# Seven-product gate/up, paired squares, early inputs and TensorE modulation in a two-layer hybrid trunk

## The chip, the cores and the metric

The kernel runs on all eight cores of one Trainium2 chip (trn2), one sequence of the batch on each core. The metric is device time in microseconds (us) of the slowest core.

A program on all cores does not always run alike on this chip. In some runs the cores of one or both dies show a lower granted clock in the records and the time is longer; such runs are called slow. In the last job below, the kernel before took 2306 to 2310 us in its fast runs, with 0.972 to 0.978 of the clock on average on every core, and 2720.5 us in its slowest, with 0.81 on one die; half_products had a run of 2399 us with 0.89 to 0.91 on one die and 0.82 to 0.83 on the other.

## The reference, cut to what matters

```python
D_MODEL, BATCH, SEQ, DEPTH, D_FF = 1024, 8, 2048, 2, 2816

def rmsnorm(x, g):
    y = x * rsqrt(mean(x * x, -1) + EPS)
    return y * g

def modulate(x, g, mod):                 # mod = silu(c) @ w_mod + b_mod, one vector per sequence
    shift, scale, gate = split(mod, 3)
    return rmsnorm(x, g) * (1 + scale) + shift, gate

def swiglu(h, w_in, w_out):
    g, u = split(h @ w_in, 2)            # 1024 -> 2 x 2816
    return (silu(g) * u) @ w_out         # 2816 -> 1024

# each layer, each with its own shift, scale and gate:
#   x += 0.5 * gate * swiglu_1(h);  x += gate * mixer(h);  x += 0.5 * gate * swiglu_2(h)
# mixer: layer 0 spatial gating and short convolution, layer 1 causal pooling; a final rmsnorm
```

Four SwiGLUs of 2048 tokens carry most of the work. A modulation vector is the product of one 1024-vector with an fp32 matrix of 1024 by 3072 per sub-layer, handled as 24 rows of 128 x 1024 (512 KB each).

## The kernel before

Tokens lie in four tiles of 512. Activations are held feature by token: a matmul has 128 x 128 weights as the stationary operand and 512 tokens as the moving one. Gate/up is the plain product, eight chunks of the inner dimension for gate and eight for up:

```python
def ffn_inproj(l, i, j, kk, t, slot, mark=False):
    ...
    for c in range(NC):                                   # NC = 8
        add("pe", I("matmul", PS[bg][:], SL[:, slot, c*256:c*256+128], role.hbuf[:, c, tsl(t)], ...))
    for c in range(NC):
        add("pe", I("matmul", PS[bu][:], SL[:, slot, c*256+128:c*256+256], role.hbuf[:, c, tsl(t)], ...))
    sg = tp_rot.next()
    add("act", I("activation", out=TP[:, sg, 0:TT], in_=PS[bg][:], func=AF.Silu), ...)
    add("dve", I("tensor_tensor", out=role.abuf[:, kk, tsl(t)], in0=TP[:, sg, 0:TT], in1=PS[bu][:], op=ALU.mult), ...)
```

The mean square over features is a matmul with a matrix of ones, one matmul for each squared chunk:

```python
def stats_gen(t, res, rot=None, sq_pool=False):
    for c in range(NC):
        ...                                               # square X[c] on GpSimd or ScalarE into SQ[q]
        add("pe", I("matmul", PS[b][:], ONES[:], SQ[:, q, :], start=(c == 0), stop=(c == NC - 1)), ...)
```

All modulation rows are dot products on VectorE, one row of 128 x 1024 a step:

```python
def mod_step():
    ...
    add("dve", I("scalar_tensor_tensor", out=JUNK[:], in0=ap, scalar=1.0, in1=CB[:],
                 op0=ALU.mult, op1=ALU.mult, accum_out=MODT[:, q:q + 1]), ...)
```

Between sub-layers a boundary works through the four tiles in turn: output projection of a tile, its squares, its sum, its normalised input for the next sub-layer.

Of the kernel before, what the change touches and what calls it, by code (L numbers as in the profile page):

```python
# [5 lines left out]
F32 = mybir.dt.float32  # L6
# [8 lines left out]
NT = 4  # L15
# [3 lines left out]
GROUPS = [list(range(0, 8)), list(range(8, 15)), list(range(15, 22))]  # L19
EPS = 1e-6  # L20
N_SUB_RUN = 6
RUN_FINAL = True

class Op:
    __slots__ = ("idx", "eng", "fn", "cdeps", "ddeps", "semkey", "pos", "seq",
                 "signal", "dma_target")

class Sched:
    ENGS = ("pe", "act", "dve", "pool", "sp")
    WINDOW = 10 ** 9  # L30

    def __init__(self):
        self.ops = []
        self.lastw = {}
        self.rd_eng = {}
        self.rd_dma = {}
        self.npos = {e: 0 for e in self.ENGS}

    def add(self, eng, fn, reads=(), writes=(), dma=None):
        ops = self.ops  # L40
        idx = len(ops)
        deps = set()
        for k in reads:
            w = self.lastw.get(k)
            if w is not None:
                deps.add(w)
        for k in writes:
            w = self.lastw.get(k)
            if w is not None:
                deps.add(w)  # L50
            r = self.rd_eng.get(k)
            if r:
                deps.update(r.values())
            r = self.rd_dma.get(k)
            if r:
                deps.update(r)
        op = Op()
        op.idx = idx
        op.eng = eng
        op.fn = fn  # L60
        op.semkey = dma
        cd = {}
        dd = []
        for d in deps:
            o = ops[d]
            if o.semkey is not None:
                dd.append(d)
            elif cd.get(o.eng, -1) < d:
                cd[o.eng] = d
        op.cdeps = cd  # L70
        op.ddeps = dd
        op.pos = self.npos[eng]
        self.npos[eng] += 1
        op.signal = False
        op.seq = 0
        op.dma_target = 0
        ops.append(op)
        for k in reads:
            if dma is not None:
                self.rd_dma.setdefault(k, []).append(idx)  # L80
            else:
                self.rd_eng.setdefault(k, {})[eng] = idx
        for k in writes:
            self.lastw[k] = idx
            self.rd_eng[k] = {}
            self.rd_dma[k] = []
        return idx

    def _skip(self, op, o):
        if o.eng == op.eng and op.semkey is None:  # L90
            if o.eng == "pe":
                return True
            if op.pos - o.pos > self.WINDOW:
                return True
        return False

    def emit(self, nc, block):
        ops = self.ops
        for op in ops:
            for e, d in op.cdeps.items():  # L100
                o = ops[d]
                if not self._skip(op, o):
                    o.signal = True
        cnt = {e: 0 for e in self.ENGS}
        dcnt = {}
        for op in ops:
            if op.semkey is not None:
                dcnt[op.semkey] = dcnt.get(op.semkey, 0) + 16
                op.dma_target = dcnt[op.semkey]
            elif op.signal:  # L110
                cnt[op.eng] += 1
                op.seq = cnt[op.eng]
        self.sig_counts = cnt
        esem = {e: nc.alloc_semaphore("s_" + e) for e in self.ENGS}
        dsem = {k: nc.alloc_semaphore("d_%d" % i) for i, k in enumerate(dcnt)}
        self.n_sems = len(esem) + len(dsem)
        by_eng = {e: [] for e in self.ENGS}
        for op in ops:
            by_eng[op.eng].append(op)

        def run(eng_name, E):
            waited = {}
            for op in by_eng[eng_name]:
                for e, d in op.cdeps.items():
                    o = ops[d]
                    if not o.signal or self._skip(op, o):
                        continue
                    if waited.get(("e", e), 0) < o.seq:
                        E.wait_ge(esem[e], o.seq)
                        waited[("e", e)] = o.seq  # L130
                for d in op.ddeps:
                    o = ops[d]
                    if waited.get(("d", o.semkey), 0) < o.dma_target:
                        E.wait_ge(dsem[o.semkey], o.dma_target)
                        waited[("d", o.semkey)] = o.dma_target
                if op.fn is None:
                    continue
                ins = op.fn(E)
                if op.semkey is not None:
                    ins.then_inc(dsem[op.semkey], 16)  # L140
                elif op.signal:
                    ins.then_inc(esem[op.eng], 1)
# [11 lines left out]

SM_BMOD = 0
# [5 lines left out]
SM_BS = 224  # L161
SM_N = 736

def _blk(w, cols):
    return np.ascontiguousarray(w[:, cols].reshape(8, 128, -1).transpose(1, 0, 2))

def piece_plan():
    plan = []
    for l in range(2):
        for i in range(2):  # L170
            if i == 1:
                if l == 0:
                    plan += [("abv", 0), ("abv", 1), ("abu", 0), ("abu", 1)]
                    for hf in range(2):
                        plan += [("abb", 2, hf), ("abb", 3, hf), ("abb", 4, hf)]
                    plan += [("abo", dp) for dp in range(4)]
                else:
                    plan += [("pool",)]
            for g, ks in enumerate(GROUPS):
                for j in ks[:4]:  # L180
                    plan.append(("win", l, i, j))
                for dp in range(4):
                    plan.append(("wout", l, i, g, dp))
                for j in ks[4:]:
                    plan.append(("win", l, i, j))
    return plan

def build_pieces(inp):
    plan = piece_plan()
    out = np.zeros((len(plan), 128, 2048), np.float32)  # L190
    w_in = inp["w_ffn_in"]
    w_out = inp["w_ffn_out"]
# [3 lines left out]
    for n, p in enumerate(plan):  # L196
        k = p[0]
        if k == "win":
            _, l, i, j = p
            w = w_in[l, i]  # L200
            a = _blk(w, slice(j * 128, (j + 1) * 128))
            b = _blk(w, slice(D_FF + j * 128, D_FF + (j + 1) * 128))
            out[n] = np.concatenate([a, b], axis=2).reshape(128, 2048)
        elif k == "wout":
            _, l, i, g, dp = p
            w = w_out[l, i]
            ks = GROUPS[g]
            blk = np.zeros((128, 2, 8, 128), np.float32)
            for dd in range(2):
                for kk, kc in enumerate(ks):  # L210
                    blk[:, dd, kk, :] = w[kc * 128:(kc + 1) * 128, (2 * dp + dd) * 128:(2 * dp + dd + 1) * 128]
            out[n] = blk.reshape(128, 2048)
        elif k == "abv":
            hp = p[1]
            out[n] = _blk(abw, slice(512 + hp * 256, 512 + (hp + 1) * 256)).reshape(128, 2048)
        elif k == "abu":
            hp = p[1]
            blk = np.stack([_blk(abw, slice((2 * hp + ff) * 128, (2 * hp + ff + 1) * 128)) for ff in range(2)], axis=1)
            out[n] = blk.reshape(128, 2048)
        elif k == "abb":  # L220
            _, sec, hf = p
            base = sec * 512
            blk = np.stack([_blk(abw, slice(base + (2 * hf + ff) * 128, base + (2 * hf + ff + 1) * 128)) for ff in range(2)], axis=1)
            out[n] = blk.reshape(128, 2048)
        elif k == "abo":
            dp = p[1]
            blk = np.stack([_blk(abo, slice((2 * dp + dd) * 128, (2 * dp + dd + 1) * 128)) for dd in range(2)], axis=1)
            out[n] = blk.reshape(128, 2048)
        elif k == "pool":
            blk = np.zeros((128, 4, 2, 256), np.float32)  # L230
            for i in range(4):
                for kc in range(2):
                    blk[:, i, kc, :] = pw[i, kc * 128:(kc + 1) * 128, :]
            out[n] = blk.reshape(128, 2048)
    return out

def build_small(inp):
# [7 lines left out]
    sm[:, SM_BS:SM_BS + 512] = np.broadcast_to(inp["ab_b_s"][0].reshape(1, 512), (128, 512))  # L245
    return sm

def build_wmod(inp):
    wm = inp["w_mod"]
    return np.ascontiguousarray(wm.transpose(0, 2, 1).reshape(2 * 72, 128, 1024))  # L250
# [3 lines left out]

def build_nc(n_sub_run=N_SUB_RUN, run_final=RUN_FINAL):
    nc = bass.Bass("TRN2", target_bir_lowering=False)
    plan = piece_plan()
    xT = nc.dram_tensor("xT", [D, S], F32, kind="ExternalInput").ap()
    cb_d = nc.dram_tensor("cb", [128, D], F32, kind="ExternalInput").ap()
    small_d = nc.dram_tensor("small", [128, SM_N], F32, kind="ExternalInput").ap()  # L260
# [915 lines left out]
```

## Time and profile before

| | before |
|---|---|
| three runs | 2306.36, 2717.41, 2721.04 us |
| the profiled run (fast) | cores 2298.5 to 2309.1 us |
| TensorE busy (slowest core) | 2151 us, 93% |
| VectorE / ScalarE / GpSimd busy | 43% / 24% / 9% |
| first gate/up matmul | 65.5 us |

The stated median of three, 2717 us, is a slow run. The fast level is 2306.

The page of the kernel before, its parts on busy time, on the 40 slices (tenths busy; PEclk is the granted clock in tenths) and on the chain that ended last:

```profile
PE 2151.3 (93%) x10136; PEld 984.7 (43%) x10136; DVE 997.4 (43%) x1575; ACT 543.1 (24%) x855; POOL 211.0 (9%) x297
...
PE   0779999999899999999999999999997699999996
...
PEclk9889999999999999999999999999997899999998
...
PE 82%; DMA 6%; DVE 4%; ACT 3%; issue 3%; SPq 1%; POOL 0%; DVEq 0%; ACTq 0%; POOLq 0%
```

The row of TensorE says where the time outside matmuls lies: in the first three slices (of 57.7 us each) and in slices 31 and 32, the pooling boundary. The same page's costliest groups (busy us, mean ns of one, idle time of the engine before them and what ended it):

```profile
L253 PE MATMUL ps<-H,SLOTS 128*128 128x512 f16 x5440 | 1198.1, 383 | 30.5 <-DMA SLOTS<-wp 19.6
L253 PE MATMUL ps<-ACTB,SLOTS 128*128 128x512 f16 x3776 | 829.8, 381 | 6.1 <-ACT ACTB L253 5.0
...
L253 DVE SCALAR_TENSOR_TENSOR JUNK<-WMOD,CB 128x1024 bf16<-128x1024 f32 x128 | 157.3, 1229 | 101.0 <-DMA WMOD<-wmod 101.0
...
L253 PE MATMUL ps<-SQ,ONES 128*128 128x512 bf16 x104 | 37.1, 421 | 67.8 <-POOL SQ L253 67.7
```

The mean of 383 ns is from start to modelled end of pipelined matmuls and is not their spacing. The spacing is read from a dense stretch. The busy time by stretch, for the same core (columns: stretch, length, busy time and count of each engine, clock, DMA share, GB/s):

```profile
65.00:180.00 115.00, 84.93 (x303) 32.35 (x304) 55.96 (x75) 39.33 (x53) 26.33 (x24) 0.81 0.57 134
1300.00:1700.00 400.00, 400.00 (x1855) 181.38 (x1854) 114.00 (x169) 47.84 (x80) 23.55 (x38) 1.00 0.24 41
1700.00:1850.00 150.00, 112.45 (x678) 59.27 (x677) 89.46 (x138) 84.50 (x123) 59.79 (x57) 0.84 0.03 5
```

In the middle line 1855 matmuls fill 400 us: 215.6 ns each. The first and third lines are the two places with holes: 30 and 38 us without a matmul.

### The profile page before, as it was taken

What the parts mean: (1) busy time and instruction counts of PE and PEld (TensorE: products, weight loads), DVE (VectorE), ACT (ScalarE), POOL (GpSimd) and SP (SyncE); (2) the same over time, 40 slices, a digit from 0 to 9 for tenths busy, and PEclk for the clock granted to TensorE, in tenths of its full rate; (3) what the DMA queues carried; (4) which work ended last, traced back from release to release, by engine and by line L of the source; (5) the groups of instructions that cost most, each with busy time, mean ns of one, the idle gap of its engine ahead of it and who ended that gap; (6) DMA issues with size and microseconds to landing.
All of it is one profiled execution on the core that took longest, in us unless ns stands there. A gap on an engine that the chain in (4) does not pass through costs nothing.

```text
span 2309.1 us, 29361 instructions; the slowest of 8 cores (2298.5 to 2309.1 us)
## 1 busy us (share of the span) xinstructions
PE 2151.3 (93%) x10136; PEld 984.7 (43%) x10136; DVE 997.4 (43%) x1575; ACT 543.1 (24%) x855; POOL 211.0 (9%) x297
## 2 busy tenths in 40 slices
PE   0779999999899999999999999999997699999996
PEld 0224444444554444444444444444444344444443
DVE  5545454315665655455426224233255612324226
ACT  1321011015422721010116310111125611010123
POOL 3500000000110000000000000000044300000000
PEclk9889999999999999999999999999997899999998
DMA  9467084230323087084430320412200041131303
GB/s 272 144 142 186 20 190 102 39 54 10 69 37 56 1 194 207 10 220 127 103 71 10 64 39 8 73 28 48 45 10 1 10 82 28 27 57 19 64 10 146
DMA packets 51375, 174.49 MB, mean 76 GB/s; under 512 B 4896, under 2 KB 4896, under 8 KB 51232
## 3 DMA queue, kind: packets, MB, share of 16 engines
q0 software_dynamic: 21744, 79.18, 20.9%
q1 hardware_dynamic: 29488, 93.45, 12.8%
q8 instruction: 85, 1.39, 0.2%
q14 instruction: 58, 0.48, 0.1%
HBM read 243.38 MB, written 8.39 MB: 109 GB/s over the span
## 4 chain that ended last, share of the span: by engine, by line
PE 82%; DMA 6%; DVE 4%; ACT 3%; issue 3%; SPq 1%; POOL 0%; DVEq 0%; ACTq 0%; POOLq 0%
PE ps L253 82%; DMA WMOD<-wmod 3%; DVE TP L253 2%; DMA SLOTS<-wp 2%; DMA X<-xT 1%; ACT H L253 1%; SPq L253 1%; DVE ACTB L253 1%; ACT TP L253 1%; DVE X L253 1%; ACT VHAT L253 0%; ACT SQ L253 0%; POOL SQ L253 0%; ACT L253 0%; DVE JUNK L253 0%
## 5 line engine op out<-in xcount | busy, mean ns | idle before, releaser
L253 PE MATMUL ps<-H,SLOTS 128*128 128x512 f16 x5440 | 1198.1, 383 | 30.5 <-DMA SLOTS<-wp 19.6
L253 PE MATMUL ps<-ACTB,SLOTS 128*128 128x512 f16 x3776 | 829.8, 381 | 6.1 <-ACT ACTB L253 5.0
L253 PEld LDWEIGHTS ps<-H,SLOTS 128*128 128x128 f16 x5440 | 534.8, 98 | 688.6 <-issue 60.8
L253 ACT ACTIVATE TP<-ps 128x512 f32<-128x512 f32 x400 | 237.0, 599 | 1468.1 <-PE ps L253 1435.6
L253 PEld LDWEIGHTS ps<-ACTB,SLOTS 128*128 128x128 f16 x3776 | 370.1, 98 | 455.5 <-issue 17.0
L253 DVE SCALAR_TENSOR_TENSOR X<-ps,GH,X 128x512 f32<-128x512 f32 x448 | 333.0, 750 | 339.1 <-PE ps L253 338.5
L253 DVE TENSOR_TENSOR ACTB<-TP,ps 128x512 f16<-128x512 f32 x280 | 192.0, 687 | 523.9 <-PE ps L253 503.0
L253 POOL DMA_DIRECT2D SLOTS<-wp x151 | 80.6, 541 | 1740.7 <-PE ps L253 1717.8
L253 DVE SCALAR_TENSOR_TENSOR JUNK<-WMOD,CB 128x1024 bf16<-128x1024 f32 x128 | 157.3, 1229 | 101.0 <-DMA WMOD<-wmod 101.0
L253 DVE TENSOR_TENSOR H<-TP,ps 128x512 f16<-128x512 f32 x88 | 60.4, 688 | 243.2 <-PE ps L253 235.9
L253 DVE TENSOR_TENSOR TP<-X,TP 128x512 f32<-128x512 f32 x192 | 135.8, 767 | 12.0 <-ACT TP L253 12.0
L253 ACT ACTIVATE H<-TP,MODT,AS 128x512 f16<-128x512 f32 x160 | 120.2, 807 | 57.6 <-DVE TP L253 57.5
L253 PE MATMUL ps<-SQ,ONES 128*128 128x512 bf16 x104 | 37.1, 421 | 67.8 <-POOL SQ L253 67.7
L253 PE MATMUL ps<-SLOTS,H 128*128 128x256 f16 x384 | 55.9, 298 | 29.2 <-ACT H L253 26.4
L253 POOL TENSOR_TENSOR SQ<-X 128x512 bf16<-128x512 f32 x56 | 70.0, 1275 | 70.3 <-PE ps L253 42.2
L253 PEld LDWEIGHTS ps<-SLOTS,H 128*128 128x128 f16 x384 | 40.0, 105 | 45.0 <-issue 38.2
L253 PEld LDWEIGHTS ps<-SQ,ONES 128*128 128x128 bf16 x104 | 10.1, 99 | 86.9 <-issue 80.2
L253 ACT ACTIVATE VHAT<-X 128x512 bf16<-128x512 f32 x64 | 38.1, 622 | 32.4 <-DVE X L253 32.4
L253 ACT ACT_TABLE_LOAD x18 | 23.1, 1283 | 72.3 <-PE ps L253 64.6
L253 POOL TENSOR_TENSOR VHAT<-X 128x512 bf16<-128x512 f32 x32 | 34.3, 1081 | 61.1 <-PE ps L253 58.0
L253 PE MATMUL ps<-VHAT,ONES 128*128 128x512 bf16 x96 | 30.2, 383 | 5.1 <-ACT VHAT L253 3.1
L253 ACT ACTIVATE SQ<-X 128x512 bf16<-128x512 f32 x48 | 27.7, 621 | 19.5 <-DVE X L253 19.3
(55 smaller groups left out, 349.7 us busy)
## 6 DMA issues: line engine op xcount, KB each, us to landing
SLOTS<-wp POOLq DMA_DIRECT2D x151, 512.0 KB, 9.0
WMOD<-wmod SPq DMA_DIRECT2D x128, 512.0 KB, 5.8
X<-xT SPq DMA_DIRECT2D x4, 2048.0 KB, 30.8
outT<-ACTB SPq DMA_DIRECT2D x4, 2048.0 KB, 7.0
ACTB<-wmod SPq DMA_DIRECT2D x8, 512.0 KB, 19.6
H<-wmod SPq DMA_DIRECT2D x8, 512.0 KB, 19.5
CB<-cb SPq DMA_DIRECT2D x1, 512.0 KB, 6.0
SM<-small SPq DMA_DIRECT2D x1, 368.0 KB, 4.3
```

The lines of the kernel that those rows point to most:

```text
L253: return lambda E: getattr(E, name)(*a, **k)
```

## The change

The intent is to do fewer matmuls and to leave TensorE no holes. Almost every line of the kernel is rewritten; in words:

1. Tokens are worked in pairs of tiles: one pair goes through a sub-layer, then the other. While a pair is in its down projection, the *other* pair's normalised input is built, so no boundary stands between them. Weights are read once per pair, so twice.
2. Gate and up for a pair of token tiles form a 2 x 2 block product (halves of the inner dimension; gate/up; two tiles). Seven quarter products replace eight. The sums of weights are 16-bit VectorE additions on the loaded weights, the sums of inputs likewise, and partial results are copied and added between PSUM banks by ScalarE and VectorE.
3. The first sub-layer's modulation (16 rows) is computed by TensorE as fp32 products with one column, eight for a row, in place of row dots on VectorE. The other rows stay on VectorE as half-rows of 512.
4. Two squares are added on GpSimd before the ones matmul: 112 ones matmuls for squares in place of 224. Ten more matmuls with the ones matrix, eight at the very beginning and two just before the first gate/up, make 122.

The diff, cut to its core (marks `...` where cut; indentation shortened):

```diff
-NT = 4
+NSLOT = 6
 ...
+def piece_sums(pc):                                     # four sums of 512-wide weight blocks, VectorE
+    tt_(v(4), v(2), v(3), ALU.add, ..., half=True)
+    tt_(v(2), v(0), v(2), ALU.subtract, ..., half=True)
+    tt_(v(5), v(4), v(0), ALU.subtract, ..., half=True)
+    tt_(v(6), v(1), v(5), ALU.subtract, ..., half=True)
+def gu_segments(units):
+    def prod(u, b, wq, hq, first):                      # one quarter product: 4 matmuls
+        for c in range(4):
+            mm(PS[b][:], SL[:, s, wq*512+c*128:wq*512+(c+1)*128], Hv4[:, hq*4+c, :], ...)
+    def P1(u):
+        prod(u, u.b1, 0, 0, True)
+        act(PS[u.b2][:], PS[u.b1][:], AF.Copy, ...)
+    def P5(u): ...
+    def P6(u):
+        prod(u, u.b2, 5, 5, False)
+        tt_(PS[u.b3][:], PS[u.b2][:], TP[:, u.p5, 0:TT], ALU.add, ...)
+    ...                                                 # P2, P7, P3, P4
-add("pe", I("matmul", PS[b][:], ONES[:], SQ[:, q, :], start=(c == 0), stop=(c == NC - 1)), ...)
+act(SQ[:, q, :], Xv(c + i, t), AF.Square, ...)          # i = 0, 1
+op = add("pool", I("tensor_tensor", out=SP[:, z, :], in0=SQ[:, qs[0], :], in1=SQ[:, qs[1], :], op=ALU.add), ...)
+mm(PS[b][:], ONES[:], SP[:, z, :], st["n"] == 0, st["n"] == NC // 2 - 1, ...)
 ...
+for t in range(2): ...                                  # squares and ones matmuls of the first pair
+for k, c in enumerate(order0):                          # then the first modulation, rows c and 8+c
+    for i in range(2):
+        for kc in range(NC):
+            op = add("pe", I("matmul", PS[b][:, i:i+1], ap[:, kc*128:(kc+1)*128], CT[:, kc:kc+1], ...))
+        if n + 9 < 16:
+            row0_dma(n + 9)                             # nine rows are under way at once
+    for tt in range(2):
+        apply_chunk(0, 0, 0, c, tt, HH)
 ...
+rstd(other, after=Sd.tl["pe"].tail())
+run_down(dn, rest, build_h(nxt))                        # the other pair's input inside the down block
```

## The prediction

> Times are for fast runs: before gave 2306, 2717 and 2721 us, and I take the two long runs for the slow state.
>
> **What bounds the kernel now.** TensorE: on the page busy 2151 of 2309 us at a mean granted clock of 0.975; the chain of waits is 82% TensorE. In the table of stretches a dense stage (1300 to 1700 us) has 1855 matmuls in 400 us: 215.6 ns per 512-column matmul at full clock. The order of instructions holds 9440 of those (9216 of weights, 224 of ones) and 58 us of narrower ones: 9440 x 0.2156 + 58 = 2093 us. The other 215 us are holes: the first 180 us hold only some 320 matmuls (loss 110; the first gate/up matmul starts at 65.5 us, then tiles wait for squares, VectorE and a weight transfer until 171), the pooling boundary at 1700 to 1850 (busy 112 of 150 us, clock 0.84; loss 45 to 60), the tail (20), and transfer waits.
>
> **What it removes.** Gate/up takes seven quarter products in place of eight: 4928 for 5632 matmuls. Paired squares leave 122 ones matmuls for 224. In all 8634 for 9440: 806 x 0.2156 = 174 us off the bound, leaving 1920 us.
>
> **What it adds.** Per gate/up unit (28 matmuls, 6.04 us): ScalarE five PSUM evacuations (599 ns each, 3.0 us); VectorE four 512-wide fp32 operations (687 ns, 2.75 us) and four 16-bit weight sums [...]. While modulation rows run, one per unit adds two 512-wide dots (about 0.8 us each): 6 us, VectorE nearly full; later 4.4 of 6. Weights are read once per token pair, so twice: 1 MB per 6 us is 175 GB/s, with a row 260, against 245 to 310 seen in the first 75 us. Tight, but buffered by six slots. On the critical path I expect 2 to 3%, about 45 us, most in the first three blocks.
>
> **Start.** 4 MB of input and 8 MB of modulation weights at 270 GB/s take 46 us. The 128 fp32 one-column products are the doubt: [...] this trace has none. Estimate 0.2 to 0.4 us each, 25 to 50 us from about 18 us on. Gate/up should start at 50 to 75 us (58) and stay dense, as no later tile's input stands in the way.
>
> **Boundaries and end.** The other pair's input is built during a down block: boundaries and pooling should leave nearly no hole. Tail 16 us.
>
> **Sum.** 1920 + 58 + 16 + 45, less 5 that the start already holds: **2034 us**, 0.88 of 2306. Range 1985 to 2110. Faster by over 2%: 0.94; within: 0.04; slower: 0.02. In the slow state the same ratio, about 2400.
>
> **What would show each step.** 8634 matmuls of 512 columns; gate/up 28 matmuls per about 6.1 us at clock 1.0; TensorE busy 95%; no stretch like 1700 to 1850; first gate/up matmul near 58 us; bandwidth near 190 GB/s; VectorE near 70% busy, above 90% in the first blocks.
>
> **What would make it wrong.** (1) fp32 products over 0.5 us each: start near 85 us. (2) VectorE or transfers limiting while rows run: the first 600 us stretch by 5 to 10%. (3) The PSUM chain of copy, add, product costing TensorE a few hundred ns per unit: 176 units x 0.3 us is 53 us. (4) Denser TensorE work lowering the granted clock in all runs; then the gain shrinks or vanishes.

The sum came to 2034 us (1920 + 58 + 16 + 45 - 5). The 0.2 to 0.4 us for an fp32 product were my estimate, with no measured product behind it, and the 58 us for the start rest on it. The 0.8 us for a 512-wide dot is near the 750 ns that VectorE's 512-wide SCALAR_TENSOR_TENSOR took in the kernel before.

## The result, and the profile after

| | before | after |
|---|---|---|
| all runs of that comparison | 2717.41, 2306.36, 2721.04, 2334.08 | 2067.70, 2066.25, 2067.11, 2067.39 |
| median | 2525.74 (two fast, two slow) | 2067.25 (all fast) |
| ratio of fast runs | | 0.8932, 95% interval 0.8869 to 0.8994 |
| TensorE busy (slowest core) | 93% | 97% |
| VectorE / ScalarE / GpSimd busy | 43 / 24 / 9% | 71 / 45 / 16% |
| HBM read | 243 MB | 392 MB |
| first gate/up matmul | 65.5 us | 81.5 us |

A ratio is the mean time of one kernel's fast runs over that of the other's of the same rounds, so it is not quite the ratio of the medians quoted. Against the fast run of 2306 the gain is 239 us; the prediction had 272.

The page of the changed kernel, the same parts and groups as above:

```profile
PE 1999.7 (97%) x9586; PEld 954.3 (46%) x9586; DVE 1470.1 (71%) x2831; ACT 922.6 (45%) x1522; POOL 329.1 (16%) x431
...
PE   6999999999999989999999999999999999999996
...
PEclk9999999999999999999999999999999999999998
...
PE 83%; DVE 13%; DMA 2%; POOL 1%; ACT 1%; issue 0%; SPq 0%; DVEq 0%; POOLq 0%
...
L323 PE MATMUL ps<-H,SLOTS 128*128 128x512 f16 x5440 | 1207.0, 380 | 17.5 <-DVE X L323 12.7
...
L323 PE MATMUL ps<-ACTB,SLOTS 128*128 128x512 f16 x3072 | 687.0, 380 | 3.2 <-DVE X L323 2.1
...
L323 POOL TENSOR_TENSOR SP<-SQ 128x512 bf16<-128x512 f32 x112 | 153.3, 1373 | 252.3 <-ACT SQ L323 236.3
...
L323 PE MATMUL ps<-SP,ONES 128*128 128x512 bf16 x122 | 48.6, 417 | 29.6 <-POOL SP L323 27.1
```

The counts are those predicted: 5440 + 3072 + 122 = 8634 matmuls of 512 columns. In TensorE's row no slice between the first and the last is under 8 tenths any more. But a full slice is not useful work by itself, as the busy time by stretch shows (same columns as before):

```profile
25.00:81.00 56.00, 55.37 (x259) 54.94 (x258) 20.12 (x74) 13.79 (x19) 7.98 (x18) 1.00 0.74 186
...
740.00:950.00 210.00, 208.56 (x966) 94.28 (x965) 148.50 (x276) 88.91 (x147) 26.41 (x37) 1.00 0.58 113
1700.00:1850.00 150.00, 148.01 (x809) 73.41 (x808) 109.43 (x177) 89.92 (x148) 32.52 (x34) 1.00 0.40 67
```

From 25 to 81 us TensorE is 99% busy with only 259 matmul records, 213 ns each. They have one column. The timeline of TensorE in that stretch (start, length, engine, operation, count):

```profile
25.83 0.58 PE L323 MATMUL ps<-SP,ONES 128*128 128x512 bf16 x1 [0.64 <-POOL SP L323]
26.21 3.41 PE L323 MATMUL ps<-CT,WMOD 128*128 128x1 f32 x16
```

and at its end:

```profile
77.27 3.55 PE L323 MATMUL ps<-CT,WMOD 128*128 128x1 f32 x16
80.68 1.07 PE L323 MATMUL ps<-SP,ONES 128*128 128x512 bf16 x2
81.55 1.91 PE L323 MATMUL ps<-H,SLOTS 128*128 128x512 f16 x4
```

The products start after the last ones matmul, at 26.2 us, and end at 80.7: 54.5 us for 128 products, 0.426 us each. The records count 256, two to a product; one such record is called a pass below. So the first part of the time beyond the prediction is here. Laid side by side, in us:

| part | predicted | after | difference |
|---|---|---|---|
| up to the first gate/up matmul | 58 | 81.5 | +24 |
| from there to the last matmul | 1960 (1920 + 45 - 5) | 1968 | +8 |
| tail | 16 | 16 | 0 |
| sum | 2034 | 2066 | +32 |

The second line comes out near the forecast, but not for its reasons, which the experiments below take apart. Its terms can be read from the trace by subtraction. After the start come 8616 of the 512-column matmuls, 1858 us at 215.6 ns. The narrower ones take 60 us by their spacing (predicted 58). That leaves 47 to 51 us, by core, in which TensorE waits; the prediction allowed 45. The profile shows 30 to 35 us of this as idle time, called visible waits below, on most cores 14.7 for VectorE's residual update (X), 11.1 for GpSimd's sum of squares (SP), 2.9 for VectorE's PSUM additions; the rest is small. It shows less than the subtraction, as the modelled end of a matmul lies 380 ns after its start where the next could start after 216, so each wait is shown too short.

### The profile page after: what moved, and what is told of

It is laid out like the page before. It is cut to its first block, busy times and chain, and to the rows that moved or that the text cites. A ratio compares the mean times of both kernels' runs of the same rounds, so it can differ in the third digit from the quotient of the medians.

```text
span 2066.1 us, 26542 instructions; the slowest of 8 cores (2061.0 to 2066.1 us)
## 1 busy us (share of the span) xinstructions
PE 1999.7 (97%) x9586; PEld 954.3 (46%) x9586; DVE 1470.1 (71%) x2831; ACT 922.6 (45%) x1522; POOL 329.1 (16%) x431
## 4 chain that ended last, share of the span: by engine, by line
PE 83%; DVE 13%; DMA 2%; POOL 1%; ACT 1%; issue 0%; SPq 0%; DVEq 0%; POOLq 0%
PE ps L323 83%; DVE X L323 4%; DVE TP L323 3%; DVE H L323 2%; DVE SLOTS L323 2%; DMA WMOD<-wmod 1%; POOL SP L323 1%; DVE WMOD L323 1%; DMA X<-xT 1%; ACT H L323 0%; ACT SQ L323 0%; DVE ps L323 0%; DVE ACTB L323 0%; ACT L323 0%; DVE MODT L323 0%
## 5 line engine op out<-in xcount | busy, mean ns | idle before, releaser
L323 PE MATMUL ps<-H,SLOTS 128*128 128x512 f16 x5440 | 1207.0, 380 | 17.5 <-DVE X L323 12.7
L323 PE MATMUL ps<-ACTB,SLOTS 128*128 128x512 f16 x3072 | 687.0, 380 | 3.2 <-DVE X L323 2.1
L323 ACT ACTIVATE ps<-ps 128x512 f32<-128x512 f32 x528 | 307.0, 583 | 666.2 <-PE ps L323 665.8
L323 DVE SCALAR_TENSOR_TENSOR X<-ps,GH,X 128x512 f32<-128x512 f32 x320 | 232.0, 746 | 132.4 <-PE ps L323 131.6
L323 DVE TENSOR_TENSOR SLOTS<-SLOTS 128x512 f16<-128x512 f16 x704 | 310.1, 459 | 10.8 <-DMA SLOTS<-win 0.9
L323 DVE TENSOR_TENSOR TP<-ps,TP 128x512 f32<-128x512 f32 x176 | 121.6, 691 | 205.9 <-ACT ps L323 205.6
L323 POOL TENSOR_TENSOR SP<-SQ 128x512 bf16<-128x512 f32 x112 | 153.3, 1373 | 252.3 <-ACT SQ L323 236.3
L323 ACT ACTIVATE SQ<-X 128x512 f32<-128x512 f32 x224 | 133.6, 622 | 118.0 <-DVE X L323 104.3
L323 DVE SCALAR_TENSOR_TENSOR WMOD<-WMOD,CB 128x512 f32<-128x512 f32 x256 | 177.6, 723 | 2.6 <-DMA WMOD<-wmod 2.5
L323 DVE TENSOR_TENSOR ps<-ps,TP 128x512 f32<-128x512 f32 x176 | 122.9, 699 | 32.7 <-PE ps L323 32.4
L323 DVE TENSOR_TENSOR TP<-X,RS 128x512 f32<-128x512 f32 x192 | 135.9, 743 | 5.5 <-ACT H L323 4.2
L323 PE MATMUL ps<-SP,ONES 128*128 128x512 bf16 x122 | 48.6, 417 | 29.6 <-POOL SP L323 27.1
```

The costliest lines, as they stand in the source:

```text
L323: return lambda E: getattr(E, name)(*a, **k)
```

## The experiments

Fifteen kernels ran, in four jobs. In each, gate/up starts are given as the range over cores. "Undisturbed cores" are those whose records show no stretch at 0.81 of the clock.

### Which part of the start is it: TensorE's products, or the arrival of rows?

My theory: the 128 products, one after another on TensorE, set the start. The rival: the rows come late. Three kernels and a control of the disputed duration itself, on one chip, on which every run of every kernel was slow (the kernel before too: 2348 to 2352 us). Only the start is read from them. A later run of the changed kernel in the slow state (as_after below) starts gate/up at 81 to 83 us, like the fast runs.

**half_products** does half the products of each row (a wrong result, relative error 0.045):

```diff
-            for kc in range(NC):
+            for kc in range(NC // 2):
```

> Only the first four of the eight fp32 products of each row of the first modulation are made (64 instead of 128; wrong result on purpose). Theory (a serial chain on TensorE: two passes of 213 ns each, 54.6 us in all, stands ahead of the first gate/up matmul): the chain is 27 us shorter, but rows still arrive until about 50 us, so gate/up starts at 55 to 60 us instead of 81.5 and the time falls from 2067 to 2040 to 2046 us. Rival (the start is set by the arrival of 8 MB of rows, the products only fill the time): start and time within 5 us of 2067.

Measured: gate/up starts at 58.5 to 60.4 us, 22 us sooner than 81.5; 64 products of 0.426 us would be 27. The products are the chain; what is left over is the arrival of rows, which the shortened chain begins to meet: on core 2 TensorE waits 4.6 us for the last three rows. (Its time, 2187.8 us median, is of slow runs and is not used.)

**f16_products** has TensorE's rows and the vector in 16 bits, cast by the DMA:

```diff
-        add("sp", I("dma_start", out=ap, in_=wmod0_d[rows0[n]]), ...)
+        add("pool", I("dma_start", out=ap, in_=wmod0_d[rows0[n]]), ...)        # ap is f16
-    ... CT[:, kc:kc + 1] ...
+    ... CT16[:, kc:kc + 1] ...
```

> The rows are cast to 16 bits on their way in, and c too, so each product is one pass in 16 bits. Theory: the chain on TensorE falls below 15 us, arrival of 12 MB becomes the bound, gate/up starts at 48 to 56 us, time 2034 to 2042 us, result still within tolerance. Rival (arrival already is the bound): within 5 us of 2067.

Measured, and correct: eight products take 0.35 us, about 44 ns each, with one record to a product. Gate/up starts at 56 to 60 us. Now the rows bind: the last ones land at 51 to 58 us, behind two weight pieces of 512 KB that were asked for ahead of them. So halving and nearly removing the products give the same start, near 59 us: the arrival was the second limit, right behind the first.

**rows_first** keeps fp32 but asks for the rows before the two input tiles, and puts the ones matmuls after 80 of the 128 products:

```diff
-    for t in range(2):
-        add("sp", I("dma_start", out=X[:, t, :, :], ...))          # from ahead of the nine rows
+    for t in range(2):
+        add("sp", I("dma_start", out=X[:, t, :, :], ...))          # to behind them
 ...
+        if k == 4:
+            ...                                                    # squares, ones matmuls, rstd, chunks 0 to 3
```

> Same products, but the rows are loaded ahead of the input, and the first eight rows' products stand ahead of the ones matmuls of the input's squares in TensorE's order. Theory: the same 54.6 us chain starts at about 6 us instead of 26, gate/up starts at 62 to 68 us, time 2048 to 2054 us. Rival (arrival of rows sets the start): the same bytes have to arrive, so the start moves by less than 5 us.

Measured, and correct: a miss. The products do start at 7 us, but gate/up starts at 75 us and is dense only from 86.5 to 86.9 (cores 7 and 2), where the changed kernel is dense from 85.1 (core 1). The input tiles now land at 31 and 39 us and the remaining rows behind them, at 43 to 53; TensorE is idle from 37 to 43 us, takes the ones matmuls at 46 to 54 and the last 48 products after them, to 75, and then gate/up waits for the sixteen normalised chunks of ScalarE and VectorE. Moving the products forward brought no earlier dense stretch by itself: the input has to come through the same transfers, and the normalisation stands behind both.

**warm_products** asks whether 0.426 us is due to a halved clock. The records of the changed kernel show 0.50 in this stretch on seven cores of the profiled run and 1.00 on one. A 512-column matmul is put ahead of every product:

```diff
             for kc in range(NC):
+                mm(PS[7][:], ONES[:], DUM[:], True, True, ["ONES", "DUM"], [("ps", 7)])
                 op = add("pe", I("matmul", ...
```

> A 512-column ones matmul stands ahead of every fp32 product, to see whether the 213 ns per pass belong to the half clock (0.50) that was granted while only one-column products ran. If a pass is clock-bound, it takes about 107 ns at full clock, a product with its filler 0.43 us, and gate/up starts near 81 us as before. If a pass takes 213 ns at any clock, a product with its filler takes 0.64 us and gate/up starts near 108 us (time about 2094). If even the fillers do not raise the clock, 0.85 us each and a start near 135 us.

Measured, and correct (three runs, outside the rounds): 0.667 us for a filler and a product on every core, and gate/up at 113 us (core 0). The timeline of TensorE, a few lines:

```profile
59.85 0.42 PE L323 MATMUL ps<-CT,WMOD 128*128 128x1 f32 x2
60.14 0.59 PE L323 MATMUL ps<-DUM,ONES 128*128 128x512 bf16 x1
60.52 0.42 PE L323 MATMUL ps<-CT,WMOD 128*128 128x1 f32 x2
```

The pair of passes starts at 59.85 and again at 60.52, and the whole step leaves about 240 ns for the filler once two passes of 213 are taken off, close to the 215.6 measured at 1.00. So the passes keep 213 ns while the filler runs at about its full-clock time. The recorded clock does not show in the times: through 27 to 113 us cores 0, 2, 3 and 6 are recorded at 1.00 and cores 1, 4, 5 and 7 at 0.50, with the same 0.667 us step. The changed kernel itself says the same: in the stretch from 26 to 80 us core 0 is recorded at 0.50 and core 1 at 1.00, with the same work:

```profile
26.00:80.00 54.00, 53.88 (x253) 53.88 (x253) 19.96 (x73) 13.09 (x18) 7.31 (x17) 0.50 0.76 185
```

```profile
26.00:80.00 54.00, 54.00 (x254) 54.00 (x254) 19.81 (x72) 12.80 (x18) 7.29 (x17) 1.00 0.74 185
```

The cost belongs to the fp32 product (0.426 us, against 44 ns in 16 bits) and not to the recorded clock. In both lines the weight-load column (the second) is as full as the matmul column; whether the load of the fp32 weights is what sets 213 ns is not shown, as no run takes the load away from the product.

### What are the seven products and the early inputs worth?

Three kernels and the changed kernel as it is, on another chip. There the changed kernel fell into short stretches at 0.812 of the clock, in all its runs:

> The changed kernel itself, as the yardstick for the runs beside it on the same chip. If this chip lets it run in the fast state: 2066 to 2068 us, as on the first chip. If the four kernels of the first job were slow because of that chip, and this is another chip, all runs here are fast; if the changed kernel draws the chip into the slow state more readily than the kernel before, it is slow here where the kernel before is not.

The spans by core of that run:

```profile
core 0: 2098.0 us, clock 0.972
core 1: 2098.6 us, clock 0.954
...
core 6: 2127.7 us, clock 0.951
core 7: 2128.7 us, clock 0.934
```

Its median is 2148 us (2130 to 2302; all but one of six slow). The records of the clock show 237 to 252 us at 0.812 in 51 to 54 stretches on cores 0 to 3 and 363 to 499 us in 24 to 33 stretches on cores 4 to 7, each time alike on a pair of cores (0 and 1, 2 and 3, and so on). What starts or ends such a stretch, no run shows. The same kernel on the first chip had none: the records of all eight cores in its profiled fast run hold 1.00 and 0.50 alone. To compare kernels on this chip I take cores 0 to 3 and subtract 0.188 (1 less 0.812) of the time at 0.812. This is an estimate and, as waits and the clock overlap, good to some 10 us: it gives 2051 for the changed kernel, which ran undisturbed at 2058 to 2066 elsewhere.

**eight_products** undoes the seven products alone: plain gate/up on the same pairs, no sums of weights or inputs, the same paired squares and early inputs.

```diff
+        for c in range(NC):
+            mm(PS[b][:], SL[:, s, wq*1024+c*128:wq*1024+(c+1)*128], HH.ap(c, tt), c == 0, c == NC - 1, ...)
-        (the seven products P1 to P7 and their copies and sums)
-    ROW_EVERY = 7
+    ROW_EVERY = 4
```

> Everything as in the changed kernel, but gate/up as eight plain products per pair of tiles, without weight sums, input sums and PSUM copies. Theory (TensorE-bound, 0.2156 us per matmul): 704 more matmuls cost 152 us, of which the relief of VectorE gives back at most 15: 2204 to 2222 us in the fast state, 1.066 to 1.075 of the changed kernel. Rival (the sums and copies of the seven-product form eat most of its gain, and the gain over the kernel before came from start and boundaries): less than 100 us slower than the changed kernel.

Measured, and correct: 2239.5 us median, fast runs 0.9656 of before (0.9625 to 0.9687). Estimated without the stretches it is 2191, against 2051 for the changed kernel by the same estimate and 2058 to 2066 where that ran undisturbed, so the seven products are worth some 130 to 140 us. The page has 704 more matmuls than after, which at 215.6 ns is 152 us:

```profile
L323 PE MATMUL ps<-H,SLOTS 128*128 128x512 f16 x6144 | 1358.3, 381 | 0.0
```

Beside the 17.5 us of idle time before this group in the changed kernel, the 0.0 here says that the seven products bring some 15 us of new visible waits with them (15 us here, 30 there). The fear of a PSUM chain that holds TensorE up for 53 us is refuted: 2.9 us of visible waits are for VectorE's PSUM additions.

**build_late** undoes the early building alone: the down block ends first, then the next input is built.

```diff
-        rstd(other, after=Sd.tl["pe"].tail())
-        run_down(dn, rest, build_h(nxt))
+        run_down(dn, rest)
+        rstd(other, after=Sd.tl["pe"].tail())
+        for _ in build_h(nxt):
+            pass
```

> The next block's input is built after the down block, not during it. Theory (boundaries are hidden by early building): at each of nine boundaries TensorE waits for rstd, sixteen normalisations at about 0.8 us of ScalarE and the input sums, 14 to 18 us, so 125 to 165 us more than the changed kernel, 2190 to 2230 us in the fast state, with nine holes in TensorE's row. Rival (engines would catch up anyway, early building is worth little): under 40 us more.

Measured, and correct: 2286.8 us median, all slow; estimated without the stretches 2205, so some 140 to 155 more than the changed kernel. Its page shows where:

```profile
L323 PE MATMUL ps<-H,SLOTS 128*128 128x512 f16 x5440 | 1280.9, 396 | 120.2 <-ACT H L323 114.5
```

TensorE waits for ScalarE's normalised input for 143 us in all, some 16 at each of nine boundaries. Inside the changed kernel this part is worth as much as the seven products: with either one undone the kernel is near 2200. The two are not shares of the gain over the kernel before, since together they exceed its 239 us. Read from eight_products, everything but the seven products brings the kernel before from 2306 to about 2191.

**combined** was a first try at a better version: 16-bit products with all 16 rows under way at once and the weights asked for later, and in addition the sums of the first two weight pieces of the next block on GpSimd.

```diff
-    for n in range(9):
+    for n in range(16):
         row0_dma(n)
-    for s, k in zip(range(NSLOT), (0, 2, 4, 5, 6, 7)):
+    for s, k in zip(range(NSLOT), (4, 6, 7, 7, 7, 7)):
         load_next(s, [gate_ops[k]])
 ...
-                    piece_sums(sum_order[k])
+                    piece_sums(sum_order[k], dn.last)              # True: on GpSimd
```

> 16-bit products for the first modulation, with all sixteen rows under way at once and ahead of the weights (the first 16-bit run showed the last rows landing at 58 us behind two weight pieces), and the weight sums of the next block's first two pieces on GpSimd. Theory: arrival of 12 MB is the bound of the start, gate/up from 48 to 54 us (81.5 in the changed kernel), the one to three us that TensorE waits at each of nine boundaries for weight sums shrink by half: 25 to 40 us less than the changed kernel beside it, 2028 to 2042 us in the fast state. Rival (something else holds the start, or GpSimd sums come too late): less than 15 us gained.

(The waits of one to three us named there are not shown as waits for weight sums: the profile of the changed kernel has 14.7 us at nine places for X and 1.6 us once for a sum.)

Measured, and correct: 2139.8 us median against 2148.3, both of slow runs; estimated without the stretches, cores 0 to 3 have 2048 to 2051 against 2051. The start is 53 us, 28 sooner, yet most of this is given back: TensorE waits 29 us for GpSimd's sums of squares, against 8 in as_after. In GpSimd's order the additional sums stood in front of the paired squares; f16_all_rows below lacks them and keeps the 28 us.

### What are the paired squares and the rows on VectorE worth?

Four kernels on a third chip, where fast runs of the changed kernel's variants came back. The control:

> The changed kernel again as yardstick on this chip: 2066 to 2068 us if it runs in the fast state, 2130 to 2160 [...]. If the last chip's slow state was a matter of that chip, a new chip may be free of it.

(The second range is that of as_after, whose cores had the stretches at 0.812.)

Fast runs 2095.4 to 2096.3. Half the cores had a single stretch of 160 us at 0.812, which cost them 30 us (160 x 0.188 = 30), and the other half spanned 2059 to 2066 us, as on the first chip. The undisturbed cores are the measure here.

**f16_all_rows** is combined without the sums on GpSimd, so the start alone.

> The combined kernel without its GpSimd sums: 16-bit products of the first modulation, all rows under way at once and ahead of the weights, weight sums back on VectorE. In the combined kernel gate/up started at 53 us, but TensorE waited 29 us for paired squares behind the sums on GpSimd, where the changed kernel beside it waited 8. Theory: start at 53 us and waits as in the changed kernel, so 25 to 30 us less than the changed kernel beside it: 2036 to 2042 us in the fast state. Rival (the later holes come with the earlier start, not with the GpSimd sums): less than 15 us gained and again over 20 us of waits for paired squares.

Measured, and correct: fast runs (four of eight) 2066.7 to 2068.2, 0.8881 of before (0.8825 to 0.8937). The cores' spans in the profiled run tell the two effects apart:

```profile
core 3: 2063.0 us, clock 0.980
core 4: 2035.4 us, clock 0.994
core 5: 2034.1 us, clock 0.993
```

Cores 4 and 5 are undisturbed, 28 us under the undisturbed cores of the control; the other six had one stretch of 160 us. The timeline of core 4's start shows the products waiting for rows, and not the reverse:

```profile
30.09 1.62 PE L323 MATMUL ps<-CTH,ACTB 128*128 128x1 f16 x48
32.93 0.35 PE L323 MATMUL ps<-CTH,ACTB 128*128 128x1 f16 x8 [1.22 <-DMA ACTB<-wmod]
...
47.11 0.35 PE L323 MATMUL ps<-CTH,WMOD 128*128 128x1 f16 x8 [0.67 <-DMA WMOD<-wmod]
...
53.39 1.91 PE L323 MATMUL ps<-H,SLOTS 128*128 128x512 f16 x4
```

**squares_single** undoes the pairing: squares are written in bf16 and each gets its own ones matmul, as in the kernel before.

```diff
         for i, q in enumerate(qs):
-            act(SQ[:, q, :], Xv(c + i, t), AF.Square, ...)
-        z = sp_rot.next()
-        op = add("pool", I("tensor_tensor", out=SP[:, z, :], in0=SQ[:, qs[0], :], in1=SQ[:, qs[1], :], op=ALU.add), ...)
-        return z, op.end + 0.3
+            op = act(SQB[:, q, :], Xv(c + i, t), AF.Square, ...)
+        return qs, op.end + 0.3
 ...
-        mm(PS[b][:], ONES[:], SP[:, z, :], ...)
+        for i, q in enumerate(z):
+            mm(PS[b][:], ONES[:], SQB[:, q, :], ...)
```

> Every squared chunk goes to its own ones matmul in 16 bits; nothing is paired on GpSimd. Theory (TensorE-bound): 112 more matmuls x 0.2156 us = 24 us, less up to 11 us of waits for paired squares that fall away: 13 to 24 us slower than the changed kernel beside it, 2080 to 2091 us in the fast state. Rival (pairing gains nothing, because TensorE waits for GpSimd instead): within 8 us.

Measured, and correct: 2056.6 us median, all runs fast, 0.8833 of before (0.8766 to 0.8900), cores 2045 to 2059. My theory, that single squares cost 13 to 24 us, fell. The groups of its page:

```profile
L323 PE MATMUL ps<-H,SLOTS 128*128 128x512 f16 x5440 | 1205.1, 380 | 5.3 <-DVE X L323 3.0
...
L323 PE MATMUL ps<-SQ,ONES 128*128 128x512 bf16 x224 | 69.5, 394 | 12.3 <-ACT SQ L323 12.1
```

There are 112 more ones matmuls (ten of the 122 stay beside these 224), 24 us of work, and still the dense part is about 10 us shorter. The idle time ahead of ones matmuls fell from 29.6 to 12.3 us, and, which I had not expected, that ahead of gate/up from 17.5 to 5.3. Visible waits in the dense part are 6 to 9 us, against 30 to 35; by the subtraction used above TensorE waits 12 to 21 us, against 47 to 51. The start gains another 2 us, as the products begin at 23.3 to 25.1 us in place of 25.5 to 26.8. On core 0:

```profile
19.54 4.22 PE L323 MATMUL ps<-SQ,ONES 128*128 128x512 bf16 x8 [2.06 <-ACT SQ L323]
23.56 3.41 PE L323 MATMUL ps<-CT,WMOD 128*128 128x1 f32 x16
```

The mechanism can be read in the changed kernel, in a boundary's timeline (bracket: idle time before, and what ended it):

```profile
1156.83 0.74 DVE L323 SCALAR_TENSOR_TENSOR X<-ps,GH,X 128x512 f32<-128x512 f32 x1
...
1157.77 0.61 ACT L323 ACTIVATE SQ<-X 128x512 f32<-128x512 f32 x1
1158.47 1.54 POOL L323 TENSOR_TENSOR SP<-SQ 128x512 bf16<-128x512 f32 x1 [4.00 <-ACT SQ L323]
1160.13 0.10 PEld L323 LDWEIGHTS ps<-SP,ONES 128*128 128x128 bf16 x1 [1.81 <-issue]
1160.16 0.38 PE L323 MATMUL ps<-SP,ONES 128*128 128x512 bf16 x1 [1.35 <-POOL SP L323]
```

From the residual update through the square to the ones matmul there is a chain, and the GpSimd sum adds 1.5 us to it; TensorE stands in order and waits 1.35 us, more than six matmuls' time, to save one. The sum is slow for what it does: mean 1373 ns, where VectorE's fp32 operation on two tiles of the same size has 743. With twice as many ones matmuls, TensorE also has work in the place where it had waited for the residual update. This last is my reading of the waits for X, 14.7 us in the changed kernel and 3 here; no run isolates it. The edit also gives the squares six buffers in place of four, so the sum itself and a shortage of buffers behind it are not told apart.

**rows_thin** takes the VectorE work of the later modulation rows away and keeps their transfers (8 columns in place of 512; a wrong result, relative error 0.445).

```diff
-                sl = slice(h * 512, (h + 1) * 512)
+                sl = slice(h * 512, h * 512 + 8)
```

> All modulation rows are still loaded, but their dots on VectorE cover 8 of 512 columns (wrong result on purpose), which takes about 170 us off VectorE, all in the first 740 us. Theory (VectorE near full there makes TensorE wait): 8 to 20 us less than the changed kernel, all before 740 us. Rival (transfers are what makes TensorE wait there): within 4 us of the changed kernel.

Measured: fast runs 2060.1 to 2060.6, cores 2053 to 2059, so 6 to 7 us under the changed kernel; visible waits 27 to 32 in place of 30 to 35. That is less than the 8 to 20 us expected and more than the rival's 4. The thinned dots still hold VectorE for 43 us (178 in the changed kernel), so most of their cost is gone, not all. VectorE's nearly full first blocks, which the prediction worried about, cost about 6 to 7 us and no 5 to 10% of 600.

### Do the two corrections add up?

The last job, on a chip that was used before, with the control again:

> The changed kernel as it is: undisturbed cores 2059 to 2067 us, first gate/up matmul at 81 to 83 us, idle about 30 us. With stretches at 0.81 of the clock on some cores: about 30 us more on those.

> Squares summed singly, the start unchanged. Theory (pairing on GpSimd is a net loss): undisturbed cores 2045 to 2059 us as on the first chip it was seen on, idle 5 to 9 us in the dense part, 6 to 12 us under as_after_third. Rival (that gain was only the other kernel's stretches at a lower clock): undisturbed cores within 3 us of those of as_after_third.

**best_both** is f16_all_rows and squares_single together.

> 16-bit products with all 16 rows under way at once, and the squares summed singly on TensorE. Theory (two separate terms that add): first gate/up matmul at 51 to 54 us, TensorE idle 5 to 10 us in the dense part, undisturbed cores span 2024 to 2032 us, i.e. 36 to 40 us under an undisturbed core of as_after_third (2059 to 2066). Rival (the start's gain and the pairing's loss are partly the same waits, or the earlier start exposes VectorE's row work): undisturbed cores at 2035 or more.

| kernel | fast runs | ratio to before | cores of the profiled run | gate/up starts |
|---|---|---|---|---|
| as_after_third | 2068.2, 2068.5, 2094.4, 2095.9 | 0.9018 (0.8963 to 0.9073) | 2061.7 to 2066.6 | 81 to 82 |
| squares_single_again | 2054.6, 2058.5, 2060.1 | 0.8914 (0.8900 to 0.8928) | 2046.7 to 2058.5 | 76 to 81 |
| best_both | 2027.6 to 2032.5 (five) | 0.8794 (0.8782 to 0.8807) | 2021.4 to 2027.9 | 51 to 54 |

No core of these three profiled runs had a stretch at 0.812, so the spans compare directly. By the median core, single squares give 14 us (2065 to 2051) and both corrections 39 (2065 to 2026): the start's 28 and the squares' 10 to 14 add up, and both theories held. The page of best_both:

```profile
PE 1964.6 (97%) x9535; PEld 915.6 (45%) x9570; DVE 1417.0 (70%) x2831; ACT 922.1 (45%) x1522; POOL 182.0 (9%) x335
...
PE 92%; DVE 3%; DMA 3%; ACT 1%; issue 0%; SPq 0%; DVEq 0%
```

The chain is 92% TensorE where it was 83%, and visible waits are 6 to 9 us. best_both is correct and is the best version, about 39 us under the changed kernel and 12% under the kernel before. It too has slow runs (three of eight: 2064, 2185 and 2316 us), as squares_single_again has (two of five: 2463 and 2466).

## Why the prediction was right or wrong

- **The bound and the counts: right.** TensorE bounds both kernels, 215.6 ns per matmul holds in both, and the 8634 matmuls are those in the trace. The seven products are worth some 130 to 140 us (eight_products), less than the 152 of their count by the waits that they bring. VectorE is 71% busy (forecast near 70), with 459 ns on average for a 16-bit weight sum against 687 for the 512-wide fp32 form.
- **"Boundaries and pooling should leave nearly no hole": right.** No slice of TensorE's row between the first and the last is under 8 tenths, where the pooling boundary had 7 and 6, and late building costs some 140 to 155 us.
- **The failed step is the start**: "Estimate 0.2 to 0.4 us each, 25 to 50 us from about 18 us on. Gate/up should start at 50 to 75 us (58)". It started at 81.5. Two terms were mis-sized. The products took 0.426 us each, 54.5 us where 58 less 18 leaves about 40: +15. And they began at 26 us in place of 18: +8 (two ones matmuls behind them add 1). The prediction named nothing that stands ahead of them. In the trace the ones matmuls of the first pair do, in TensorE's order: the second input tile lands at 19.4 us (core 1), and then its squares, pair sums and ones matmuls follow. The pair sums are about 2 us of these 8, as squares_single shows. half_products and f16_products show that the serial products were the limit, and f16_all_rows that 28 us come back with 16-bit products and all rows under way at once.
- **The paired squares: wrong in sign.** "Paired squares leave 122 ones matmuls for 224" was counted as part of the 174 us, 22 us of gain. It costs 10 to 14 us (squares_single twice, on two chips). The saving in matmuls is real (112, 24 us), but it brings about 33 us of waits (47 to 51 us in all, against 12 to 21): the GpSimd sum lies on the chain between the residual update and TensorE.
- **The allowance of 45 us for waits** was about enough, by luck: 47 to 51 us by subtraction. It was meant mostly for the first three blocks, where VectorE's row work cost 6 to 7 us (rows_thin), and about 33 us of it were used up by the paired squares, which stood in the sum as a gain.
- **"In the slow state the same ratio, about 2400": not borne out.** It came from reading the slow state as one fixed level of 2717. It is no fixed level: slow runs of the kernel before lie from 2348 to 2721 us and those of the changed kernel as it is from 2114 to 2302, with the slow die's mean granted clock at 0.81 in the slowest of them and at 0.96 in the mildest. The stated 2717 median is a draw from that mixture; what the change is worth is read from fast runs, which show 10.7% off the time.
- The risk named first, "fp32 products over 0.5 us each: start near 85 us", had the right place and the wrong threshold: 0.43 us with a later beginning came to almost the same start. The risk named last, a lower granted clock in all runs, did not come on that chip: the cores' means are 0.972 to 0.994 in the four runs after, against 0.973 to 0.977 in the profiled run before.

What stays open: why the changed kernel meets stretches at 0.812 in one run and on one chip and not in another. The chip alone does not decide it: the first job, where every run was slow, and the last, where most were fast, ran on the same chip. Fast profiles of it without any such stretch (twice) and with one of 160 us on half of the cores exist for the same code, so no part of the change needs it as an explanation.

## What to carry to other kernels

Cost a new serial piece at the start by a duration measured for that very form (type and shape), and look up what stands ahead of it in the engine's own order; a 99% busy engine may be doing 54 us of work that 16 bits do in 6. Before moving a sum off the limiting engine, ask what chain it lies on: here 1.4 us on GpSimd replaced 0.2 us of TensorE and was waited for. When two mis-sized terms of opposite sign meet an allowance, the total may look almost right, so take the terms apart by single undos.
